# Attention of the meta tokens in layer 0: eight heads at a time in blocks of 16, instead of four in blocks of 32

## The chip, the cores and the metric

The kernel runs on one core of a Trainium2 chip. The metric is the time of one execution in microseconds on the device. The engines of a core work side by side, each through its own instructions in order: PE (matrix products), DVE (vector work), ACT (functions of one operand, and scaled copies), POOL (general work) and SP, which here only starts transfers.

## The reference

The reference is a decoder of two layers over 272 tokens (16 learned meta tokens, then 256 of the sequence), width 2048, 16 heads of 128. Layer 0 uses forgetting attention; the queries are taken in blocks, and the first block is the 16 meta tokens:

```
bounds = [(0, N_META)]                                  # 16 meta tokens
for start in range(N_META, total_len, BLOCK): ...       # then blocks of 128
s = einsum('bqhd,bkhd->bhqk', q[:, qs:qe], k[:, :qe]) * scale
s = s + cum_logf[:, :, qs:qe, None] - cum_logf[:, :, None, :qe]
p = softmax(where(k_pos <= q_pos, s, -inf))
o = einsum('bhqk,bkhd->bqhd', p, v[:, :qe])
```

So of every head the meta block is a product of 16 queries with 16 keys, a sum with differences of the forget gates, a softmax, and a product with 16 values. Then come the output projection and a squared-ReLU MLP of width 8192; layer 1 uses stick-breaking attention over keys and values shared from layer 0's output, and an MLP of its own. All is float32.

## The kernel before

Activations lie feature-major, x[feature, token], in 16 chunks of 128 features. Every large product (qkv, output projections, MLPs, shared k/v: 96 groups) runs through `gemm_group`: 512 columns of weights, four blocks `kb` of 512 features each. A block arrives as two halves `raw`; ACT writes each half rounded to the PE's faster float type (`whi`, L235), DVE writes what is left over (`wlo`, L236), and PE does three products for each pair of weight tile and chunk: whi with x's upper part, whi with its lower part, wlo with the upper part (L177). In layer 0 the moving operand is 272 columns wide, in most of layer 1 it is 256.

In layer 0 the heads go in four groups `g` of four heads. Each group has a q, a k and a v product; the attention's small work is put among them by hand through `before`, `after` and `mid`, and by a scheduler which orders the rest from a model of its own. `behind` fixes a small matmul behind the last large one, so that it stands at a set place in the PE's queue.

What concerns the meta tokens, for one group of four heads:

- L600: `packed` lets POOL copy the first 32 query columns of each head to a 128-column tile `qm`.
- `meta` (L603) runs ahead of block 2 of the v product. One full float32 matmul of `qm` with the first 32 key columns of four heads gives a 128x128 tile `ps0`, in which only the four 32x32 blocks on the diagonal count (L605); DVE makes the decays `s0` from the gates `fk`, the column `fqm_sb` and the mask `maskM` (L608), adds and takes the minimum (L610); ACT takes the exponential (L612); DVE divides (L613, L614).
- After the v product the first 32 value columns are turned to token-major: for groups 0 to 2 by DVE and 16 copies shared by ACT and POOL (`turned_corners`, L523 and L528; the last 16 keys of each 128-token block go along), for group 3 by two PE transposes (L635).
- `small` (L630) runs ahead of block 2 of the next product (of block 1 in the output projection): DVE turns the probabilities (L639), one full float32 matmul multiplies them with the values (`pom`, L641), and `put_split` writes the 16 real columns of four heads to the attention's output `ao` (L642).

`outputs` (L483) does the 128-token blocks; for group 3 it stands in the middle of block 2 of the first group of the output projection. Its matmuls `po` need the probabilities' parts `ph`, `pl` and the values' parts `vs` (upper part by ACT, L448, lower part by DVE, L449). The gates of the meta queries come from four small transfers that ACT starts (`meta_gates`, L373).

The activations `x` live in two buffers of 16 rows of 640 columns and 64 columns more.

Of the kernel before, what the change touches and what calls it, by code (L numbers as in the profile page):

```python
# [21 lines left out]
EPS = 1e-6  # L22
BIG = 1.0e30
# [4 lines left out]
SPAN = 6  # L28
WIDE = {"o1": (0, 4, 10)}
XROW = 640  # L30
# [6 lines left out]
def yoco_kernel(ctx: ExitStack, tc: tile.TileContext, hT_in, gains, b_f, w_f, w_qkv0, w_o0, w_up, w_dn,  # L37
                w_kv, w_q1, w_o1, g_fin, out):
    nc = tc.nc

    const = ctx.enter_context(tc.tile_pool(name="const", bufs=1))
# [4 lines left out]
    xs = ctx.enter_context(tc.tile_pool(name="xs", bufs=2))  # L46
    tmp = ctx.enter_context(tc.tile_pool(name="tmp", bufs=2))
# [19 lines left out]
    for _ in range(9):  # L67
# [12 lines left out]
    nc.gpsimd.affine_select(out=maskM, in_=maskM, compare_op=ALU.is_ge, fill=BIG, base=0,  # L80
                            pattern=[[-32, 4], [-1, 32]], channel_multiplier=1)
    nc.gpsimd.affine_select(out=maskM, in_=maskM, compare_op=ALU.is_ge, fill=BIG, base=31,
                            pattern=[[32, 4], [0, 32]], channel_multiplier=-1)


    maskB = const.tile([P, 416], F32, name="maskB")
# [18 lines left out]
    class Split:  # L105


        def __init__(self, label, t0):
            n = T - t0
            self.t0 = t0  # L110
            rows = xs.tile([P, NC * XROW + 64], F32R, tag="x", name=f"x_{label}")
            hi, lo = ROWS[t0]
            o = min(hi, lo)
            rows = rows[:, o:o + NC * XROW].rearrange("p (c t) -> p c t", c=NC)
            self.hi, self.lo = (rows[:, :, k - o:k - o + n] for k in (hi, lo))

            if t0:
                self.wide = {}
                self.wide_chunks = WIDE.get(label, (0,))
                for c in self.wide_chunks:  # L120
                    for name, k in (("hi", hi), ("lo", lo)):
                        nc.gpsimd.tensor_copy(rows[:, c, k - o + n:k - o + n + SPAN], pad[:, :SPAN])
                        self.wide[name, c] = rows[:, c, k - o:k - o + n + SPAN]

    def split_chunk(sp, gi, c):

# [177 lines left out]
    xa = Split("a0", 0)  # L304
# [14 lines left out]
            norm.add(c)  # L319

    fq_sb = const.tile([P, 2, NC], F32, name="fq_sb")
    fqm_sb = const.tile([P, 4], F32, name="fqm_sb")
    f_dram = tc.dram_tile([NC, T], F32, name="f_dram")

    def load_gates():
        wf_sb = att.tile([P, NC, NC], F32, tag="qs", name="wf_sb")
        wf = att.tile([P, NC, 2 * NC], F32, tag="qs", name="wf")
        for t, n, c, out, src in ((wf_sb[:, 0], P, 13, wf_sb, w_f), (bf_sb, NC, 14, bf_sb, b_f),
                                  (g_sb[:, 0], P, 15, g_sb, gains)):
            nc.gpsimd.tensor_copy(t[:n, :1], hT[:n, c, :1])  # L330
            nc.gpsimd.dma_start(out, src)
        nc.vector.memset(wf, 0.0)
        nc.vector.tensor_tensor(out=wf[:, :, :NC], in0=wf_sb, op=ALU.mult,
                                in1=g_a0.unsqueeze(2).to_broadcast([P, NC, NC]))
        both = att.tile([P, P], F32, tag="pk", bufs=3, name="both")[:, :NC]
# [33 lines left out]

    def meta_gates():  # L370

        for g in range(4):
            nc.scalar.dma_start(fqm_sb[:, g:g + 1], f_dram[4 * g:4 * g + 4, :32].rearrange("h (t o) -> h t o", o=1))  # L373

    def split_q(q, label):

# [127 lines left out]
    def packed(src, label):  # L504

        n = src.shape[2]
        t = att.tile([P, P], F32, tag="pk", bufs=3, name=f"pk_{label}")[:, :4 * n]
        nc.gpsimd.tensor_copy(t.rearrange("p (h t) -> p h t", h=4), src)
        return t

    def corners(a, b, label):

        t = att.tile([P, P], F32, tag="pk", bufs=3, name=f"pk_{label}")
        for i, src in enumerate((a, b)):
            nc.gpsimd.tensor_copy(t.rearrange("p (h c t) -> p h c t", h=4, c=2)[:, :, i, :], src)
        return t

    def turned_corners(parts, out, label):

        n = len(parts)  # L520
        ct = tmp.tile([P, T], F32, tag="u2", name=f"ct_{label}")[:, :n * P].rearrange("p (s k) -> p s k", s=n)
        for i, src in enumerate(parts):
            nc.vector.transpose(out=ct[:, i], in_=src)  # L523
        out = out.rearrange("p (s k) -> p s k", s=n)
        for a in range(0, P, 32):
            for b in range(0, P, 32):
                copy = nc.scalar.copy if n == 2 and a < 64 else nc.gpsimd.tensor_copy
                copy(out[b:b + 32, :, a:a + 32], ct[a:a + 32, :, b:b + 32])  # L528

    def last_keys(vT):  # L530

        return vT[:, :, M:].rearrange("p h (c t) -> p h c t", c=2)[:, :, :, P - M:]

    def put_split(sp, h, nh, t, n, src):
        hi, lo = (x[:, h:h + nh, t - sp.t0:t - sp.t0 + n] for x in (sp.hi, sp.lo))
        nc.scalar.activation(hi, src, AF.Copy)
        nc.vector.tensor_tensor(out=lo, in0=src, in1=hi.bitcast(F32), op=ALU.subtract)
# [3 lines left out]
    for g in range(4):  # L541
# [55 lines left out]
            for i, (o, n) in enumerate(((0, 144), (144, T))):  # L597
                nc.vector.tensor_scalar(s[:, j, o:o + n], s[:, j, o:o + n], st[:, 2 + i:3 + i], None, op0=ALU.mult)

        qm = packed(qT[:, :, :32], f"qm_{g}")  # L600
        s0 = tmp.tile([P, T], F32, tag="sq", name=f"s0_{g}")[:, :P]

        def meta(g=g, qm=qm, kT=kT, s0=s0, fk=fk, last=box["s"]):  # L603
            ps = patt.tile([P, 512], F32, tag="patt", name=f"ps0_{g}")
            behind(nc.tensor.matmul(ps[:, :P], qm, kT[:, :, :32], start=True, stop=True))  # L605
            st = att.tile([P, 4], F32, tag="st", name=f"st0_{g}")
            with tc.issue_after(last.ins):
                nc.vector.scalar_tensor_tensor(out=s0.rearrange("p (h k) -> p h k", h=4), in0=fk[:, :, :32],  # L608
                                               scalar=fqm_sb[:, g:g + 1], in1=maskM, op0=ALU.subtract, op1=ALU.add)
# [8 lines left out]

        vT, evac_v = values(f"0_{g}")
        plan = PLANS[0 if g else 2]  # L620
        gemm_group(w_qkv0[3 * g + 2], xa, 0, evac_v, {2: meta}, early(turn_p[0], plan[0]))

        if g == 3:
            vm, vc = packed(vT[:, :, 0:32], f"vm_{g}"), corners(vT[:, :, P:144], vT[:, :, 256:T], f"vc_{g}")
# [5 lines left out]
        def small(g=g, corner=(vm, vc) if g == 3 else None, vm_sb=vm_sb, sm=sm, s0=s0, box=box):  # L630
# [10 lines left out]
            behind(nc.tensor.matmul(po[:, :P], vm_sb[:, :P], pm_sb[:, P:], start=True, stop=True))  # L641
# [192 lines left out]

    def last_down(f, u):

        home = xs.tile([P, NC * XROW + 64], F32R, tag="x", name="home")[:, :8 * 1152].rearrange(
            "p (q h w k c) -> p q h w k c", q=2, h=2, w=2, k=2)
        for g in range(4):
            pool, tag = ((patt, "patt"), (pacc, "acc"))[g % 2]  # L840
# [82 lines left out]
```

## Time and profile before

| | |
|---|---|
| median of 3 runs | 2260.46 us (2260.19 to 2261.04) |
| the profiled execution | 2261.43 us, of which 2259.70 us are the span from its first to its last instruction |
| PE | 2250.6 us busy, 18845 matmuls |
| DVE | 1390.7 us busy (62%) |
| ACT | 1125.6 us busy (50%) |
| POOL | 112.4 us busy (5%) |
| memory | 408.33 MB read, 182 GB/s over the span |
| layer 0's attention and its projections | roughly the first 410 us |

A group of the profile is one line of the program on one engine with the tiles it writes and reads; behind the count stand the busy time, the mean length of one, and the idle time of the engine ahead of it. The length of a matmul reaches from its start to its end in the array, and the next one starts before that end; so what a matmul costs in a dense stream is read from the starts of its neighbours. A float32 matmul counts as two.

### The profile page before, as it was taken

Reading aid. Unit: us, or ns where it says so; the run is one execution under the profiler, and the core shown is the slowest. Engines: PE = TensorE matmul, PEld = TensorE weight load, DVE = VectorE, ACT = ScalarE, POOL = GpSimd, SP = SyncE. Lnnn points to the kernel's source line nnn. Section 1 sums busy time; section 2 is a strip of 40 time slices with the busy share of each in tenths; the row PEclk is TensorE's granted clock in tenths of the full one; section 3 lists DMA queues with packets and bytes.
Section 4 is the critical chain, followed back from the end, with each engine's and each line's share of the span. In section 5 each row is a group of like instructions: output and inputs, shape, how many; then the busy total and the mean of one; then the engine's idle time right before and its main releaser. Section 6 shows DMA issues by size and latency. Waiting matters only on the chain.

```text
span 2259.7 us, 44965 instructions
## 1 busy us (share of the span) xinstructions
PE 2250.6 (100%) x18845; PEld 2247.4 (99%) x18845; DVE 1390.7 (62%) x1997; ACT 1125.6 (50%) x1577; POOL 112.4 (5%) x220
## 2 busy tenths in 40 slices
PE   9999999999999999999999999999999999999998
PEld 9999999999999999999999999999999999999998
DVE  7877786554455455445566688876555555555655
ACT  6664565443344344344544577755543544543543
POOL 1000000000000000000000010100000000001421
PEclk9999999999999999999999999999999999999999
DMA  7545545555555555555555544466656656565564
GB/s 245 183 158 176 182 160 176 182 174 177 185 173 183 178 169 186 171 184 179 175 187 187 177 163 160 168 203 187 202 183 203 194 188 201 183 204 193 187 200 150
DMA packets 116507, 413.37 MB, mean 183 GB/s; under 512 B 13456, under 2 KB 15776, under 8 KB 116304
## 3 DMA queue, kind: packets, MB, share of 16 engines
q1 hardware_dynamic: 113904, 406.25, 55.4%
q8 instruction: 147, 2.41, 0.5%
q10 hardware_dynamic: 2000, 3.03, 0.4%
q0 software_dynamic: 400, 1.21, 0.1%
q14 instruction: 56, 0.46, 0.1%
HBM read 408.33 MB, written 2.11 MB: 182 GB/s over the span
## 4 chain that ended last, share of the span: by engine, by line
PE 99%; DMA 1%; DVE 0%; ACT 0%; issue 0%; DVEq 0%; ACTq 0%
PE acc L177 93%; PE acc_t L293 4%; DMA raw<-w_qkv 1%; PE ps L400 1%; PE po L495 1%; PE ps L398 0%; PE po L498 0%; DMA rows<-hT_in 0%; PE pf L344 0%; DVE wlo L236 0%; PE pc L486 0%; DVE x_a L132 0%; DVE ssq_a L149 0%; ACT x_a L131 0%; ACT whi L235 0%; PE ps L605 0%
## 5 line engine op out<-in xcount | busy, mean ns | idle before, releaser
L236 DVE TENSOR_TENSOR wlo<-raw,whi 128x1024 fp32r<-128x1024 f32 (+1 forms) x742 | 891.0, 1218 | 605.6 <-ACT whi L235 599.4
L235 ACT ACTIVATE whi<-raw 128x1024 fp32r<-128x1024 f32 (+1 forms) x742 | 764.5, 1050 | 881.7 <-PE acc L177 847.6
L177 PE MATMUL acc<-x_m,whi 128*128 128x272 f32 (+1 forms) x4096 | 642.6, 281 | 0.0
L177 PE MATMUL acc<-x_u,whi 128*128 128x272 f32 (+1 forms) x3584 | 576.6, 282 | 0.0
L177 PEld LDWEIGHTS acc<-x_m,whi 128*128 128x128 f32 x4096 | 565.7, 188 | 0.0
L177 PEld LDWEIGHTS acc<-x_u,whi 128*128 128x128 f32 x3584 | 504.0, 188 | 0.0
L177 PE MATMUL acc<-x_m,wlo 128*128 128x272 f32 (+1 forms) x2048 | 440.7, 281 | 0.0
L177 PE MATMUL acc<-x_u,wlo 128*128 128x272 f32 (+1 forms) x1792 | 403.9, 282 | 0.0
L177 PE MATMUL acc<-x_a,whi 128*128 128x272 f32 (+1 forms) x2048 | 352.8, 285 | 0.1
L177 PEld LDWEIGHTS acc<-x_m,wlo 128*128 128x128 f32 x2048 | 323.2, 188 | 0.0
L177 PEld LDWEIGHTS acc<-x_a,whi 128*128 128x128 f32 x2048 | 300.2, 188 | 1.3 <-issue 0.9
L177 PEld LDWEIGHTS acc<-x_u,wlo 128*128 128x128 f32 x1792 | 290.7, 188 | 0.0
L177 PE MATMUL acc<-x_a,wlo 128*128 128x272 f32 (+1 forms) x1024 | 252.8, 285 | 0.3 <-DVE wlo L236 0.3
L177 PE MATMUL acc<-x_kv,whi 128*128 128x272 f32 x1024 | 192.4, 287 | 0.0
L177 PEld LDWEIGHTS acc<-x_a,wlo 128*128 128x128 f32 x1024 | 175.6, 188 | 0.7 <-DVE wlo L236 0.7
L177 PE MATMUL acc<-x_o,whi 128*128 128x272 f32 (+2 forms) x1024 | 162.0, 282 | 0.0
L177 PEld LDWEIGHTS acc<-x_kv,whi 128*128 128x128 f32 x1024 | 160.0, 188 | 0.0
L177 PE MATMUL acc<-x_kv,wlo 128*128 128x272 f32 x512 | 147.1, 287 | 0.0
L177 PEld LDWEIGHTS acc<-x_o,whi 128*128 128x128 f32 x1024 | 141.8, 188 | 0.0
L177 PE MATMUL acc<-x_o,wlo 128*128 128x272 f32 (+1 forms) x512 | 110.2, 281 | 0.0
L300 DVE TENSOR_TENSOR rows<-acc,rows 128x272 f32<-128x272 f32 (+1 forms) x144 | 62.3, 433 | 74.1 <-PE acc L177 74.1
L177 PEld LDWEIGHTS acc<-x_kv,wlo 128*128 128x128 f32 x512 | 96.4, 188 | 0.0
(216 smaller groups left out, 1521.8 us busy)
## 6 DMA issues: line engine op xcount, KB each, us to landing
raw<-w_up SPq DMA_DIRECT2D x256, 512.0 KB, 3.9
raw<-w_dn SPq DMA_DIRECT2D x224, 512.0 KB, 3.7
raw<-w_qkv SPq DMA_DIRECT2D x92, 512.0 KB, 3.9
raw<-w_o SPq DMA_DIRECT2D x64, 512.0 KB, 4.0
raw<-w_kv SPq DMA_DIRECT2D x64, 512.0 KB, 3.8
raw<-w_q SPq DMA_DIRECT2D x32, 512.0 KB, 4.4
raw_t<-w_dn SPq DMA_DIRECT2D x32, 512.0 KB, 4.3
fk<-f_dram ACTq DMA_DIRECT2D x4, 544.0 KB, 5.5
```

The source lines that it names most:

```text
L177: ins = nc.tensor.matmul(*args, **kw).ins
L235: on_act = nc.scalar.activation(hp, src, AF.Copy)
L236: on_dve = nc.vector.tensor_tensor(out=lp, in0=src, in1=hp.bitcast(F32), op=ALU.subtract)
L293: ins = nc.tensor.matmul(accs[b][h][:, :256 + over], x[:, 4 * kb + kc, b * P:(b + 1) * P], parts[kc // 2][w][:, kc % 2, 256 * h:256 * h + ...
L300: nc.vector.tensor_tensor(out=hT[:, c, t0:], in0=acc, in1=hT[:, c, t0:], op=ALU.add)
L400: nc.tensor.matmul(ps[:, 144:416], qs[a][:, j, :], ks[b][:, j, :], start=i == 0, stop=i == 2)
L495: ins = nc.tensor.matmul(po[:, i, :], vk, pk, start=i == k == 0, stop=False)
```

## The change

The meta attention is done for two groups of four heads together, in 16-column blocks of eight heads, in the odd groups alone. Tiles `qm`, `km`, `vm` and `s0` of 8 x 16 columns are made once for a pair of groups; POOL fills their halves from `qT`, `kT` and `vT` (three copies of 64 columns a group, where one of 128 stood). The even groups keep only their half of the decays. So `ps0`, the softmax, the turning of values and probabilities, `pom` and `put_split` stand twice and not four times. In even groups `turned_corners` has one part and not two; its 16 copies then all go to POOL. `meta_gates` starts two transfers, not four. The pool `pk` has two buffers, not three, and the 64 spare columns of an `x` buffer go, so that the second `x` buffer starts 256 bytes earlier in a partition; the columns used within a buffer stay the same.

```diff
-    maskM = const.tile([P, 4, 32], F32, name="maskM")
+    maskM = const.tile([P, 8, M], F32, name="maskM")
...
-            rows = xs.tile([P, NC * XROW + 64], F32R, tag="x", name=f"x_{label}")
+            rows = xs.tile([P, NC * XROW], F32R, tag="x", name=f"x_{label}").rearrange("p (c t) -> p c t", c=NC)
             hi, lo = ROWS[t0]
-            o = min(hi, lo)
-            rows = rows[:, o:o + NC * XROW].rearrange("p (c t) -> p c t", c=NC)
-            self.hi, self.lo = (rows[:, :, k - o:k - o + n] for k in (hi, lo))
+            self.hi, self.lo = (rows[:, :, k:k + n] for k in (hi, lo))
...
-        for g in range(4):
-            nc.scalar.dma_start(fqm_sb[:, g:g + 1], f_dram[4 * g:4 * g + 4, :32].rearrange("h (t o) -> h t o", o=1))
+        for g in range(2):
+            nc.scalar.dma_start(fqm_sb[:, g:g + 1], f_dram[8 * g:8 * g + 8, :M].rearrange("h (t o) -> h t o", o=1))
...
-        qm = packed(qT[:, :, :32], f"qm_{g}")
-        s0 = tmp.tile([P, T], F32, tag="sq", name=f"s0_{g}")[:, :P]
-
-        def meta(g=g, qm=qm, kT=kT, s0=s0, fk=fk, last=box["s"]):
+        if g % 2 == 0:
+            qm, km, vm, s0 = (att.tile([P, 8, M], F32, tag=f"meta_{x}", bufs=1, name=f"{x}_{g}") for x in ("qm", "km", "vm", "s0"))
+        four = slice(4 * (g % 2), 4 * (g % 2) + 4)
+        nc.gpsimd.tensor_copy(qm[:, four], qT[:, :, :M])
+        nc.gpsimd.tensor_copy(km[:, four], kT[:, :, :M])
+
+        def meta_decays(g=g, s0=s0, fk=fk, last=box["s"], four=four):
+            with tc.issue_after(last.ins):
+                nc.vector.scalar_tensor_tensor(out=s0[:, four], in0=fk[:, :, :M], scalar=fqm_sb[:, g // 2:g // 2 + 1],
+                                               in1=maskM[:, four], op0=ALU.subtract, op1=ALU.add)
+
+        def meta(g=g, qm=qm, km=km, s0=s0, decays=meta_decays):
             ps = patt.tile([P, 512], F32, tag="patt", name=f"ps0_{g}")
-            behind(nc.tensor.matmul(ps[:, :P], qm, kT[:, :, :32], start=True, stop=True))
+            behind(nc.tensor.matmul(ps[:, :P], qm, km, start=True, stop=True))
...
-        gemm_group(w_qkv0[3 * g + 2], xa, 0, evac_v, {2: meta}, early(turn_p[0], plan[0]))
-
+        gemm_group(w_qkv0[3 * g + 2], xa, 0, evac_v, {2: meta if g % 2 else meta_decays}, early(turn_p[0], plan[0]))
+
+        nc.gpsimd.tensor_copy(vm[:, four], vT[:, :, :M])
...
-            turned_corners([vT[:, :, 0:32], last_keys(vT)], vm_sb, f"0_{g}")
+            turned_corners([vm, last_keys(vT)] if g % 2 else [last_keys(vT)], vm_sb if g % 2 else vm_sb[:, P:], f"0_{g}")
...
-            nc.vector.transpose(out=pm_sb[:, P:], in_=s0)
+            if g % 2 == 0:
+                return
+            nc.vector.transpose(out=pm_sb[:, P:], in_=s0.rearrange("p h k -> p (h k)"))
             po = patt.tile([P, 512], F32, tag="patt", name=f"pom_{g}")
             behind(nc.tensor.matmul(po[:, :P], vm_sb[:, :P], pm_sb[:, P:], start=True, stop=True))
-            put_split(ao, 4 * g, 4, 0, M, po[:, :P].rearrange("p (h q) -> p h q", h=4)[:, :, :M])
+            put_split(ao, 4 * g - 4, 8, 0, M, po[:, :P].rearrange("p (h q) -> p h q", h=8))
```

On PE, `ps0` and `pom` of the groups 0 and 2 are gone, and nothing stands in their place. Beside the instructions that go, the scheduler moves others at two places, shown below; the remaining order on PE is the same. On DVE and ACT a few more rows move in groups 1 and 2 (the turned values' copies on ACT stand behind `ph` in group 1, and DVE turns `vm` four rows after the last keys). The names below carry the numbers of a build; `acc_13` is the first group of the output projection, and the first number behind `whi` or `wlo` is that of the product (3 is the v product of group 0), the second its block, the third the half.

On ACT, from the gates' transfers of group 0 into its v product, before:

```order
L373 DMA fqm_sb_138<-f_dram_141 128x1x1 x4
L389 ACTIVATE kh0_0_581<-kT0_0_580 128x272 x3
L235 ACTIVATE whi_3_1_0_976<-raw_3_1_0_972 128x1024
L235 ACTIVATE whi_3_1_1_980<-raw_3_1_1_973 128x1024
L389 ACTIVATE kh0_0_581<-kT0_0_580 128x272
L235 ACTIVATE whi_3_2_0_1044<-raw_3_2_0_1040 128x1024
L235 ACTIVATE whi_3_2_1_1048<-raw_3_2_1_1041 128x1024
L594 ACTIVATE s_0_579,st_0_852<-s_0_579,st_0_852 128x144
L594 ACTIVATE s_0_579,st_0_852<-s_0_579,st_0_852 128x272
L594 ACTIVATE s_0_579,st_1_865<-s_0_579,st_1_865 128x144
L594 ACTIVATE s_0_579,st_1_865<-s_0_579,st_1_865 128x272
```

and now:

```order
L371 DMA fqm_sb_138<-f_dram_141 128x1x1 x2
L387 ACTIVATE kh0_0_579<-kT0_0_578 128x272 x3
L233 ACTIVATE whi_3_1_0_977<-raw_3_1_0_973 128x1024
L233 ACTIVATE whi_3_1_1_981<-raw_3_1_1_974 128x1024
L387 ACTIVATE kh0_0_579<-kT0_0_578 128x272
L592 ACTIVATE s_0_577,st_0_850<-s_0_577,st_0_850 128x144
L233 ACTIVATE whi_3_2_0_1038<-raw_3_2_0_1034 128x1024
L592 ACTIVATE s_0_577,st_0_850<-s_0_577,st_0_850 128x272
L592 ACTIVATE s_0_577,st_1_863<-s_0_577,st_1_863 128x144
L592 ACTIVATE s_0_577,st_1_863<-s_0_577,st_1_863 128x272
L233 ACTIVATE whi_3_2_1_1042<-raw_3_2_1_1035 128x1024
```

Two of the four transfers go, and the halves of block 2 now stand among the exponentials of the scores instead of ahead of them; DVE's subtraction `wlo_3_2_1` likewise moves behind the divisions of the first two heads, and the first score product with `kh` moves 10 large matmuls forward on PE.

On PE, in the middle of block 2 of the output projection's first group, where `outputs` of group 3 stands, before:

```order
L486 MATMUL pc_0_3_4213<-pm_sb_0_3_4083,vm_sb_3_4003 128x128
L177 MATMUL acc_13_0_4006<-x_o0_142,whi_13_2_1_4176 128x272 x2
L177 MATMUL acc_13_0_4006<-x_o0_142,wlo_13_2_1_4177 128x272
L177 MATMUL acc_13_0_4006<-x_o0_142,whi_13_2_1_4176 128x272 x2
L177 MATMUL acc_13_0_4006<-x_o0_142,wlo_13_2_1_4177 128x272
L177 MATMUL acc_13_1_4007<-x_o0_142,whi_13_2_1_4176 128x272
L495 MATMUL po_0_3_0_4216<-ph_0_3_4110,vs_0_3_4186 128x256
L495 MATMUL po_0_3_0_4216<-pl_0_3_4111,vs_0_3_4186 128x256
L495 MATMUL po_0_3_1_4228<-ph_0_3_4110,vs_0_3_4186 128x256
L495 MATMUL po_0_3_1_4228<-pl_0_3_4111,vs_0_3_4186 128x256
```

and now:

```order
L484 MATMUL pc_0_3_4191<-pm_sb_0_3_4061,vm_sb_3_3981 128x128
L493 MATMUL po_0_3_0_4194<-ph_0_3_4088,vs_0_3_4164 128x256
L493 MATMUL po_0_3_0_4194<-pl_0_3_4089,vs_0_3_4164 128x256
L493 MATMUL po_0_3_1_4206<-ph_0_3_4088,vs_0_3_4164 128x256
L493 MATMUL po_0_3_1_4206<-pl_0_3_4089,vs_0_3_4164 128x256
L175 MATMUL acc_13_0_3984<-x_o0_142,whi_13_2_1_4154 128x272 x2
L175 MATMUL acc_13_0_3984<-x_o0_142,wlo_13_2_1_4155 128x272
L175 MATMUL acc_13_0_3984<-x_o0_142,whi_13_2_1_4154 128x272
L493 MATMUL po_0_3_0_4194<-ph_0_3_4088,vs_0_3_4164 128x256
L496 MATMUL po_0_3_0_4194<-pt_0_3_3708,vt_0_3_3980 128x128
```

The four `po` matmuls that use the upper part of `vs` follow `pc` at once, where 7 large matmuls stood between; the first `po` that uses the lower part of `vs` (the ninth row) now has 4 large matmuls ahead of it since `pc`, where it had 16.

More of the change, by code (lines that the diff above doesn't have):

```diff
@@ L76, in yoco_kernel @@
                             base=M + P, pattern=[[-1, T]], channel_multiplier=1)
-    maskM = const.tile([P, 4, 32], F32, name="maskM")
+    maskM = const.tile([P, 8, M], F32, name="maskM")
     nc.gpsimd.memset(maskM, 0.0)
     nc.gpsimd.affine_select(out=maskM, in_=maskM, compare_op=ALU.is_ge, fill=BIG, base=0,
-                            pattern=[[-32, 4], [-1, 32]], channel_multiplier=1)
-    nc.gpsimd.affine_select(out=maskM, in_=maskM, compare_op=ALU.is_ge, fill=BIG, base=31,
-                            pattern=[[32, 4], [0, 32]], channel_multiplier=-1)
+                            pattern=[[-M, 8], [-1, M]], channel_multiplier=1)
+    nc.gpsimd.affine_select(out=maskM, in_=maskM, compare_op=ALU.is_ge, fill=BIG, base=M - 1,
+                            pattern=[[M, 8], [0, M]], channel_multiplier=-1)
     maskB = const.tile([P, 416], F32, name="maskB")
@@ L121, in __init__ @@
                     for name, k in (("hi", hi), ("lo", lo)):
-                        nc.gpsimd.tensor_copy(rows[:, c, k - o + n:k - o + n + SPAN], pad[:, :SPAN])
-                        self.wide[name, c] = rows[:, c, k - o:k - o + n + SPAN]
+                        nc.gpsimd.tensor_copy(rows[:, c, k + n:k + n + SPAN], pad[:, :SPAN])
+                        self.wide[name, c] = rows[:, c, k:k + n + SPAN]
     def split_chunk(sp, gi, c):
@@ L321, in yoco_kernel @@
     fq_sb = const.tile([P, 2, NC], F32, name="fq_sb")
-    fqm_sb = const.tile([P, 4], F32, name="fqm_sb")
+    fqm_sb = const.tile([P, 2], F32, name="fqm_sb")
     f_dram = tc.dram_tile([NC, T], F32, name="f_dram")
@@ L506, in packed @@
         n = src.shape[2]
-        t = att.tile([P, P], F32, tag="pk", bufs=3, name=f"pk_{label}")[:, :4 * n]
+        t = att.tile([P, P], F32, tag="pk", bufs=2, name=f"pk_{label}")[:, :4 * n]
         nc.gpsimd.tensor_copy(t.rearrange("p (h t) -> p h t", h=4), src)
@@ L511, in corners @@
     def corners(a, b, label):
-        t = att.tile([P, P], F32, tag="pk", bufs=3, name=f"pk_{label}")
+        t = att.tile([P, P], F32, tag="pk", bufs=2, name=f"pk_{label}")
         for i, src in enumerate((a, b)):
@@ L598, in yoco_kernel @@
                 nc.vector.tensor_scalar(s[:, j, o:o + n], s[:, j, o:o + n], st[:, 2 + i:3 + i], None, op0=ALU.mult)
-        qm = packed(qT[:, :, :32], f"qm_{g}")
-        s0 = tmp.tile([P, T], F32, tag="sq", name=f"s0_{g}")[:, :P]
-        def meta(g=g, qm=qm, kT=kT, s0=s0, fk=fk, last=box["s"]):
+        if g % 2 == 0:
[8 more added lines that the diff above has]
+        def meta(g=g, qm=qm, km=km, s0=s0, decays=meta_decays):
             ps = patt.tile([P, 512], F32, tag="patt", name=f"ps0_{g}")
-            behind(nc.tensor.matmul(ps[:, :P], qm, kT[:, :, :32], start=True, stop=True))
+            behind(nc.tensor.matmul(ps[:, :P], qm, km, start=True, stop=True))
             st = att.tile([P, 4], F32, tag="st", name=f"st0_{g}")
-            with tc.issue_after(last.ins):
-                nc.vector.scalar_tensor_tensor(out=s0.rearrange("p (h k) -> p h k", h=4), in0=fk[:, :, :32],
-                                               scalar=fqm_sb[:, g:g + 1], in1=maskM, op0=ALU.subtract, op1=ALU.add)
+            decays()
+            s0 = s0.rearrange("p h k -> p (h k)")
             nc.vector.tensor_tensor_reduce(out=s0, in0=ps[:, :P], in1=s0, scale=1.0,
@@ L627, in yoco_kernel, with small @@
         if g < 3:
-            turned_corners([vT[:, :, 0:32], last_keys(vT)], vm_sb, f"0_{g}")
-        def small(g=g, corner=(vm, vc) if g == 3 else None, vm_sb=vm_sb, sm=sm, s0=s0, box=box):
+            turned_corners([vm, last_keys(vT)] if g % 2 else [last_keys(vT)], vm_sb if g % 2 else vm_sb[:, P:], f"0_{g}")
+        def small(g=g, corner=(vm.rearrange("p h k -> p (h k)"), vc) if g == 3 else None, vm_sb=vm_sb, sm=sm, s0=s0, box=box):
             box["pm"] = pm_sb = corner_probs(sm, f"0_{g}")
@@ L835, in last_down @@
     def last_down(f, u):
-        home = xs.tile([P, NC * XROW + 64], F32R, tag="x", name="home")[:, :8 * 1152].rearrange(
+        home = xs.tile([P, NC * XROW], F32R, tag="x", name="home")[:, :8 * 1152].rearrange(
             "p (q h w k c) -> p q h w k c", q=2, h=2, w=2, k=2)
```

4 lines of the change are left out of this document (2 added, 2 removed).

## The prediction

> **What bounds the kernel now.** I read the cores' view first, then the page's busy times and chain, then PE's waits.
>
> ```profile
> core 0: 2259.7 us, clock 0.999
> PE 2250.6 (100%) x18845; PEld 2247.4 (99%) x18845; DVE 1390.7 (62%) x1997; ACT 1125.6 (50%) x1577; POOL 112.4 (5%) x220
> PE 99%; DMA 1%; DVE 0%; ACT 0%; issue 0%; DVEq 0%; ACTq 0%
> PE idle L68 <- DVE mean_w L62: 1.1, 1, 1.1
> PE acc L177 <- DVE wlo L236: 0.3, 1, 0.3
> ```
>
> PE is the bound: 99% of the chain that ends last is PE, it runs at its full granted clock (0.999), and its waits on other engines add up to 1.4 us. Time is won only by taking instructions out of PE's queue or by starting them closer together, and lost only if PE now waits for something or its matmuls start further apart. The meta tokens' work on DVE (62% busy), ACT (50%) and POOL (5%) costs nothing in itself.
>
> The profiled execution took 2261.43 us, of which 2259.70 are the span; the median of the runs shown, 2260.46, is 0.97 lower. I make the sum as a difference against the profiled execution and take it off the median.
>
> **What leaves PE.** Four full float32 matmuls go: `ps0` and `pom` of the groups 0 and 2. Of each of these two rows of the profile half goes:
>
> ```profile
> L641 PE MATMUL pom<-pm_sb,vm_sb 128*128 128x128 f32 x8 | 1.5, 272 | 0.0
> L605 PE MATMUL ps<-kT,pk_qm 128*128 128x128 f32 x8 | 1.5, 272 | 0.0
> ```
>
> Each matmul counts twice, so 8 records are four matmuls. What one costs is read from the starts around it, here in group 0's v product:
>
> ```profile
> 71.77 0.29 PE L177 MATMUL acc<-x_a,wlo 128*128 128x272 f32 x1
> ...
> 72.14 0.29 PE L177 MATMUL acc<-x_a,wlo 128*128 128x272 f32 x1
> 72.27 0.38 PE L605 MATMUL ps<-kT,pk_qm 128*128 128x128 f32 x2
> 72.40 0.50 PE L177 MATMUL acc<-x_a,whi 128*128 128x272 f32 x2
> 72.74 0.29 PE L177 MATMUL acc<-x_a,wlo 128*128 128x272 f32 x1
> 72.87 0.41 PE L177 MATMUL acc<-x_a,whi 128*128 128x272 f32 x2
> 73.11 0.29 PE L177 MATMUL acc<-x_a,wlo 128*128 128x272 f32 x1
> ```
>
> From one `wlo` to the next stand three large matmuls, 72.14 - 71.77 = 0.37 us (0.123 each); the stretch with `ps0` takes 72.74 - 72.14 = 0.60. So one small matmul costs 0.23 us of PE. `pom` has the same shape and the same 272 ns. Four of them are **-0.92 us**, all on the path, because PE never rests there.
>
> The Trainium skill (TensorE: Matmul & The Clock Gate, "Wait — 56ns, not 53.3ns?") has N / 2.4 GHz + about 2.5 ns for one warm matmul in a stream, 56 ns at 128 columns. By that page two passes would be 0.11 us and the four matmuls 0.45 us, an estimate, and the forecast 0.47 us later. The row above has twice that, and I take the row.
>
> **What is moved on PE, in the output projection.** `outputs` of group 3 now stands tighter behind `pc`. First PE, then DVE, then ACT, before the change:
>
> ```profile
> 329.35 0.38 PE L486 MATMUL pc<-pm_sb,vm_sb 128*128 128x128 f32 x2
> 329.49 0.49 PE L177 MATMUL acc<-x_o,whi 128*128 128x272 f32 x2
> ...
> 330.44 0.28 PE L495 MATMUL po<-ph,vs 128*128 128x256 f32 x1
> 330.56 0.28 PE L495 MATMUL po<-pl,vs 128*128 128x256 f32 x1
> ...
> 332.03 0.28 PE L495 MATMUL po<-ph,vs 128*128 128x256 f32 x1
> ...
> 332.29 0.36 PE L495 MATMUL po<-ph,vs 128*128 128x256 f32 x1
> 332.49 0.28 PE L495 MATMUL po<-pl,vs 128*128 128x256 f32 x1
> ...
> 334.87 0.46 PE L177 MATMUL acc<-x_o,whi 128*128 128x272 f32 x2
> ```
>
> ```profile
> 327.80 1.23 DVE L236 TENSOR_TENSOR wlo<-raw,whi 128x1024 fp32r<-128x1024 f32 x1
> 328.94 0.22 DVE L537 TENSOR_TENSOR x_o<-pom,x_o 128x64 fp32r<-128x64 f32 x1
> 329.07 1.22 DVE L236 TENSOR_TENSOR wlo<-raw,whi 128x1024 fp32r<-128x1024 f32 x1
> 330.20 0.69 DVE L449 TENSOR_TENSOR vs<-vt,vs 128x512 fp32r<-128x512 f32 x1
> ```
>
> ```profile
> 327.86 0.63 ACT L448 ACTIVATE vs<-vt 128x512 fp32r<-128x512 f32 x1 [0.34 <-DVE vt L441]
> ```
>
> The upper part of `vs` is there at 327.86 + 0.63 = 328.49, so the first four `po` may follow `pc` at once. The lower part comes at 330.20 + 0.69 = 330.89; DVE is dense ahead of it, and the row `x_o<-pom` now has 128 columns for 64, which I put at 0.07 more (a subtraction of 1024 columns takes 330.20 - 329.07 = 1.13 from start to start, so 64 take 0.07): 330.96. PE needs that part at the fifth `po`. In the old order that was 332.03, with 1.1 us to spare. In the new one it is 329.35, plus 0.14 for `pc` (329.49 - 329.35), 0.20 for the first `po` behind a float32 matmul (332.49 - 332.29), 3 x 0.12 for the next three (330.56 - 330.44) and 4 x 0.123: 330.54. All these times hang on the end of group 3's v product and move together. For handing over between the engines I allow 0.05; no row shows PE waiting for DVE at such a place. PE waits 330.96 + 0.05 - 330.54 = **+0.47 us**, with all later matmuls behind it.
>
> Something comes back. The old order has PE held a little at block 3, which needs what `outputs` wrote: the pair at 334.87 lasts 0.46, against 0.41 for a pair elsewhere (at 72.87). In the new one the `po` end about 0.9 us earlier, less the wait, and that hold goes: **-0.05**. The bounds of this part are 0 (the part arrives in time) and +0.6 (handing over takes 0.15).
>
> **What is moved in group 0.** The chain there starts with ACT:
>
> ```profile
> 54.78 3.13 ACTq L373 DMA_DIRECT2D fqm_sb<-f_dram  x4
> 57.96 1.07 ACT L389 ACTIVATE kh<-kT 128x272 fp32r<-128x272 f32 x3 [5.26 <-DMA fqm_sb<-f_dram]
> ...
> 61.02 0.38 PE L400 MATMUL ps<-kh,qh 128*128 128x272 f32 x1
> ```
>
> ```profile
> 65.68 0.30 DVE L591 CUSTOM_DVE_ANT_0 s<-ps,s 128x144 f32<-128x144 f32 x1
> ...
> 66.86 2.36 DVE L236 TENSOR_TENSOR wlo<-raw,whi 128x1024 fp32r<-128x1024 f32 x2
> 69.13 0.41 DVE L596 RECIPROCAL st<-st 128x2 f32<-128x2 f32 x2
> 69.46 1.03 DVE L598 TENSOR_SCALAR s<-s,st 128x144 f32<-128x144 f32 x4
> ```
>
> Starting the four transfers keeps ACT for 3.13 us; two take about half, so `kh` can come some 1.5 us earlier. The first product with `kh` stands 10 x 0.123 = 1.2 us earlier on PE, near 59.8; even the old `kh` starts at 57.96 and its first third is done by about 58.4. No wait. The second half of block 2, `wlo_3_2_1`, was done at 66.86 + 2.36 = 69.22. It now follows the divisions (0.41 + 1.03) and one more head's pair of score rows, about 0.6 (two heads take 66.86 - 65.68 = 1.18), and its `whi` stands behind exponentials; with 1 us more for those it is done by 72.3. PE needs it 24 large matmuls into block 2, at 72.40 + 24 x 0.123 = 75.35, less 0.23. I take 0, with 3 us of cover; if the cover were gone, each late half would be paid in full, +0.5 to +1.5.
>
> **What costs nothing.** The 64-column copies on POOL (5% busy) lie a whole product ahead of `ps0` and `pom`; DVE's turning of `vm` in group 1 waits for POOL, with the subtractions of the weights queued behind it, but four turns of the values stand ahead of it as cover. If POOL came later than these, DVE's slack on the weights would pay first.
>
> **The sum.** -0.92 + 0.47 - 0.05 = -0.50 us. Against the profiled execution that is 2260.93; off the median, 2260.46 - 0.50 = **2260.0 us**. That is 0.02%, far inside the 0.2% (4.5 us) that a measurement of this kernel can tell from no change.
>
> **The rivals.**
>
> *The lower part of `vs` is in time.* If DVE's dense stretch ahead of it ends 0.5 us sooner, the whole saving stays: -0.92 - 0.05, 2259.5. For it: DVE loses small work in the groups 0 and 2. Against it: in group 3 its rows are as many as before. Chance 0.22.
>
> *Group 0 stalls.* If the exponentials hold up `whi` longer than I allow, PE waits for `wlo` in block 2 or 3: 2260.5 to 2261.5. For it: ACT and DVE are reordered there most. Against it: 3 us of cover. Chance 0.09.
>
> *POOL holds up DVE.* In groups 0 and 2 POOL now makes 16 copies where it made 8:
>
> ```profile
> 86.66 3.10 POOL L528 COPY vm_sb<-ct 32x64 f32<-32x64 f32 x8 [10.06 <-DVE ct L523]
> ```
>
> Eight took 3.10 us beside DVE's subtractions. Were DVE to stand still for as long in each of the two groups, it would lose some 3 us twice, about the cover that I found for the weights in group 0; PE might pay 0.5, giving 2260.5. It decides only where the loss exceeds that cover. Chance 0.04. The Trainium skill (SBUF — State Buffer, "Who interferes with whom") states the rule that speaks for this: a DVE instruction with two SBUF inputs contends with a GpSimd instruction that reads SBUF, and the later one waits. The row agrees that something waits: eight copies in 3.10 us are 0.39 each; it does not show DVE waiting.
>
> *Matmuls start further apart: slower.* The second `x` buffer moves by 256 bytes, and PE has a slower gait, seen in layer 1 behind a float32 matmul:
>
> ```profile
> 1469.99 1.08 PE L177 MATMUL acc<-x_o,whi 128*128 128x262 f32 x8
> 1470.90 0.27 PE L769 MATMUL pvc<-ident,pk_vc 128*128 128x128 f32 x1
> 1470.93 1.19 PE L177 MATMUL acc<-x_o,whi 128*128 128x262 f32 x8
> 1471.96 1.09 PE L177 MATMUL acc<-x_o,wlo 128*128 128x262 f32 x8
> ...
> L177 PE MATMUL acc<-x_m,whi 128*128 128x256 f32 x2032 | 262.5, 276 | 0.0
> ```
>
> Eight matmuls ahead of `pvc` take 1470.90 - 1469.99 = 0.91 (0.114 each); the eight behind it 1471.96 - 1470.93 = 1.03, of which the first is 0.20, so the others 0.118 each: 0.0045 more. It outweighs the saving from about 110 matmuls on and shows in the time from 1,000 on. Should layer 1's up projections, which read the second buffer (the 2032 of the last row and half as many with `wlo`), keep that gait throughout, they cost 3048 x 0.0045 = 14 us: 2274. Against it: the gait ended within those eight, and the columns within a buffer stay. Chance 0.04. The same shift could as well bring starts closer together (0.03 for faster by over 0.2%), though no row shows a quicker gait.
>
> **How the numbers follow.** 2260.0 has 0.58; the rivals 0.22, 0.09, 0.04, 0.04 and 0.03. The first four cases all lie within 0.2%: same 0.93, slower 0.04, faster 0.03. The range covers 2259.5 less, and 2261.5 more, some 0.4 to 0.7 for the scatter of the runs (2260.19 to 2261.04): 2258.8 to 2261.9.
>
> **What would show it.** Right: `ps0` and `pom` with x4 records each; 0.37 us between `wlo` starts across block 2 of group 0; one new wait of PE, `po` for DVE's `vs`, near 0.5 us; the first pair of block 3 at 0.41. Wrong: no such wait (the first rival), a wait of `acc` for `wlo` below 90 us (the second) or in the groups' next products (the third), or more than 0.125 between the large matmuls of 272 columns, 0.115 of 256, over hundreds of them.

## The result, and the profile after

| | before | after |
|---|---|---|
| median of 22 runs each | 2260.47 us (2259.34 to 2261.91) | 2263.34 us (2261.41 to 2265.57) |
| ratio after / before | | 1.0014, 95% interval 1.0007 to 1.0020 |
| profiled execution's span | 2259.70 us | 2261.5 us |

The changed kernel is 2.9 us slower, where the forecast was 0.5 us faster. The removal itself took place. The groups of the profile show `ps0` and `pom` with half their records:

```profile
L611 PE MATMUL ps<-km,qm 128*128 128x128 f32 x4 | 0.8, 274 | 0.0
L649 PE MATMUL pom<-pm_sb,vm_sb 128*128 128x128 f32 x4 | 0.8, 272 | 0.0
```

The cores' view and the page's busy times of the changed kernel:

```profile
core 0: 2261.5 us, clock 0.998
PE 2249.9 (99%) x18837; PEld 2246.9 (99%) x18837; DVE 1387.7 (61%) x1983; ACT 1120.4 (50%) x1555; POOL 129.7 (6%) x243
```

PE is busy 0.7 us less and yet the span is longer. What PE waits for (engine, tile and line, what it waits for; then us in total, times, longest):

```profile
PE acc L175 <- DVE x_o L535: 2.6, 1, 2.6
PE idle L68 <- DVE mean_w L62: 1.1, 1, 1.1
```

The first row is new: one stop of 2.6 us, on a large matmul that needs what DVE writes into `x_o`. It has its place in the timeline of PE, at the start of block 2 of the output projection's first group (start, length, instruction; in brackets how long PE stood idle ahead of it, and what ended that):

```profile
321.60 0.38 PE L649 MATMUL pom<-pm_sb,vm_sb 128*128 128x128 f32 x2
...
323.92 0.28 PE L175 MATMUL acc<-x_o,whi 128*128 128x272 f32 x1
326.82 0.39 PE L175 MATMUL acc<-x_o,whi 128*128 128x272 f32 x1 [2.62 <-DVE x_o L535]
327.06 0.28 PE L175 MATMUL acc<-x_o,wlo 128*128 128x272 f32 x1
...
328.33 0.66 PE L175 MATMUL acc<-x_o,whi 128*128 128x272 f32 x2
328.79 0.43 PE L175 MATMUL acc<-x_o,wlo 128*128 128x272 f32 x1
329.01 0.66 PE L175 MATMUL acc<-x_o,whi 128*128 128x272 f32 x2
```

DVE and ACT at the same place:

```profile
322.62 2.69 DVE L439 STREAM_TRANSPOSE vt<-vT 32x256 f32<-32x256 f32 x6
325.35 1.23 DVE L234 TENSOR_TENSOR wlo<-raw,whi 128x1024 fp32r<-128x1024 f32 x1
326.49 0.28 DVE L535 TENSOR_TENSOR x_o<-pom,x_o 128x128 fp32r<-128x128 f32 x1
```

```profile
322.02 0.28 ACT L534 ACTIVATE x_o<-pom 128x128 fp32r<-128x128 f32 x1
```

`pom` of group 3 is done near 322.0, and ACT writes the upper part at once. The lower part stands on DVE behind six turns and a subtraction of weights and is done at 326.49 + 0.28 = 326.77. The second matmul of block 2 reads it and starts at 326.82 in place of 323.92 + 0.12 = 324.04: 2.78 us late. Block 2 holds the features 1024 to 1535, which are heads 8 to 11. Before the change their meta columns came from group 2, and DVE had written them 72 us earlier:

```profile
254.26 0.22 DVE L537 TENSOR_TENSOR x_o<-pom,x_o 128x64 fp32r<-128x64 f32 x1
```

Now one `put_split` writes heads 8 to 15 together, when group 3 is ready.

The stop has a second cost. In the timeline, three large matmuls take 329.01 - 328.33 = 0.68 us, where three took 0.37. The table by stretches (length; busy time and count of PE, its weight loads PEld, DVE, ACT, POOL; PE's granted clock; share and GB/s of the transfers) shows why:

```profile
326.82:328.17 1.35, 1.34 (x11) 1.35 (x12) 1.35 (x2) 0.00 (x0) 0.00 (x0) 1.00 0.40 94
328.22:331.63 3.41, 3.41 (x17) 3.41 (x17) 0.28 (x1) 0.51 (x1) 0.00 (x0) 0.50 0.78 272
```

From 328.22 on, 1.40 us behind the stop, PE has half its clock for 3.41 us, and each large matmul costs 0.227 us in place of 0.123.

Both traces have the same 18,432 large matmuls in the same order, so the start of each in one trace can be taken from its start in the other. The table gives how this distance to the first trace of before grows in each stretch (us; negative is ahead; times are those of before), for all kernels of this study:

| trace | to 46 us | 46 to 326.4 | 326.4 to 326.7 (the stop) | 326.7 to 336 | 336 to 1470 | 1470 to 1490 | to the end |
|---|---|---|---|---|---|---|---|
| after | -1.55 | -0.91 | +2.89 | +1.50 | 0.00 | 0.00 | -0.28 |
| e0, after again | -1.55 | -0.91 | +3.05 | +1.14 | 0.00 | 0.00 | -0.28 |
| before again | -1.24 | 0.00 | 0.00 | 0.00 | +0.01 | 0.00 | -0.28 |
| e1, early write | -0.31 | -0.91 | 0.00 | +0.51 | 0.00 | 0.00 | -0.28 |
| e4, half as late | -1.47 | -0.91 | +1.75 | -0.06 | 0.00 | 0.00 | -0.28 |
| e5, late write alone | -1.46 | 0.00 | +2.94 | +1.48 | 0.00 | +1.55 | -0.28 |
| e3, early write, late po | -1.82 | -0.91 | 0.00 | -0.09 | 0.00 | 0.00 | -0.28 |
| e6, groups 0 and 1 only | -1.25 | -0.45 | 0.00 | 0.00 | +0.01 | 0.00 | -0.28 |
| e7, filler, first execution | +0.09 | -0.91 | +2.42 | +1.30 | 0.00 | 0.00 | -0.28 |
| e7, second execution | -1.07 | -0.91 | +2.24 | +1.49 | 0.00 | 0.00 | -0.28 |
| e7, third execution | -0.23 | -0.91 | +2.25 | -0.06 | 0.00 | +1.37 | -0.28 |
| e4, second execution | -1.09 | -0.91 | +1.75 | -0.07 | 0.00 | +1.04 | -0.28 |

The first, the sixth and the last column belong to single executions: the second trace of the unchanged kernel differs from its first one by 1.24 and 0.28 there. What the change did lies in the three columns between: -0.91 for the four matmuls, and +4.38 (after) or +4.19 (e0) at block 2. Whether the change also moves the start by some tenths of a microsecond, these single executions cannot tell.

### The profile page after: what moved, and what is told of

Its sections match the earlier page's. It is cut to its first block, busy times and chain, and to the rows that moved or that the text cites. A ratio compares the mean times of both kernels' runs of the same rounds, so it can differ in the third digit from the quotient of the medians.

```text
span 2261.5 us, 44929 instructions
## 1 busy us (share of the span) xinstructions
PE 2249.9 (99%) x18837; PEld 2246.9 (99%) x18837; DVE 1387.7 (61%) x1983; ACT 1120.4 (50%) x1555; POOL 129.7 (6%) x243
## 4 chain that ended last, share of the span: by engine, by line
PE 85%; DVE 0%; ACT 0%; DVEq 0%; issue 0%
PE acc L175 80%; PE acc_t L291 4%; PE po L493 0%; PE ps L398 0%; PE po L496 0%; PE ps L396 0%; PE pc L484 0%; DVE hrow L840 0%; DVE hrow L838 0%; DVE hrow L811 0%; DVE sqr L814 0%; ACT sums L824 0%; DVEq L927 0%; PE pms_m L156 0%; PE pms_m L155 0%; DVE sums L827 0%
```

## The experiments

**e0: the changed kernel again.**

> The changed kernel once more, unaltered. Theory: block 2 of the first group of the output projection reads heads 8 to 11 of the attention's output, whose meta columns are now written together with those of heads 12 to 15, late; PE stops 2.7 us there and then runs some 3 us at half its clock (+1.5 us). Expected 2262.3 to 2264.5, the same stop near 326.8 us, and the stretch at half clock either there again or begun at another moment. Rival: the time is spread over the whole run, and the stop or the half clock does not come back.

2263.18 us against 2260.25 (ratio 1.0012, 1.0003 to 1.0021). The stop is there again, of the same length. So is the half clock, but it begins at 326.44, while PE still stands, and not 1.40 us behind the stop, so that the first matmul is slow already:

```profile
326.44:326.82 0.38, 0.00 (x1) 0.01 (x1) 0.38 (x3) 0.00 (x0) 0.00 (x0) 0.50 0.18 75
```

```profile
326.82 0.59 PE L175 MATMUL acc<-x_o,whi 128*128 128x272 f32 x1 [2.61 <-DVE x_o L535]
327.21 0.43 PE L175 MATMUL acc<-x_o,wlo 128*128 128x272 f32 x1
```

The loss belongs to the kernel, not to one execution.

**e1: the late write moved ahead, alone.** The lower part of the meta output goes ahead of the last six turns and of block 3's weights on DVE. The `po` are fixed on PE where the changed kernel has them, so that PE's and ACT's order are the same as there.

```diff
-            put_split(ao, 4 * g - 4, 8, 0, M, ...)
+            box["mo"] = put_split(ao, 4 * g - 4, 8, 0, M, ...)   # returns the lower part's instruction
...
+        if g == 3:
+            def last_turns(piece=turning[2]):
+                with tc.issue_after(box["mo"].ins):
+                    piece()
+            turning[2] = last_turns
...
+                        if hold and kb == 3:                     # first group of the output projection
+                            held.enter_context(tc.issue_after(hold["mo"].ins))
                         on_dve = nc.vector.tensor_tensor(out=lp, in0=src, in1=hp.bitcast(F32), op=ALU.subtract)
```

> The changed kernel with one row moved on DVE: the lower part of the meta output of heads 8 to 15 is written two entries (six turns of the values and one subtraction of weights) earlier. PE's and ACT's order stay. Theory: the write is done near 322.9, block 2 starts unheld at 324.05, there is no half clock, and what is left is the wait of the first lower po for vs that the prediction named, 0.3 to 0.5: 2260.46 - 0.92 + 0.4 = 2259.9 (2259.3 to 2260.8). Rival, the loss lies elsewhere (copies on POOL, addresses, start): about 2263. Rival, the wait moves on to what was moved back (weights of block 3, vs): 2261 to 2262.

2259.67 us against 2260.25 (0.9997, 0.9989 to 1.0006). One row of DVE moved by two entries takes back the whole loss: 3.5 us between e0 and e1, measured side by side. Its waits:

```profile
PE idle L68 <- DVE mean_w L62: 1.1, 1, 1.1
PE po L517 <- DVE vs L456: 0.3, 1, 0.3
PE acc L175 <- DVE wlo L241: 0.3, 1, 0.3
```

The stop at block 2 is gone; the last row is one that a trace of before has too. What comes up is the wait that the prediction named, on PE and DVE:

```profile
329.20 0.29 PE L175 MATMUL acc<-x_o,whi 128*128 128x272 f32 x1
329.80 0.39 PE L517 MATMUL po<-ph,vs 128*128 128x256 f32 x1 [0.32 <-DVE vs L456]
330.03 0.38 PE L518 MATMUL po<-pt,vt 128*128 128x128 f32 x2
```

```profile
323.74 0.29 DVE L580 TENSOR_TENSOR x_o<-pom,x_o 128x128 fp32r<-128x128 f32 x1
...
329.06 0.69 DVE L456 TENSOR_TENSOR vs<-vt,vs 128x512 fp32r<-128x512 f32 x1
```

The first lower `po` starts 0.60 us behind the matmul ahead of it, where 0.12 is usual: 0.48 us, with `vs` done at 329.75 and 0.05 for handing over. The next start comes 0.23 later and not 0.12, another 0.11.

**e4: half as late.** As e1, but the write stands behind the six turns and only ahead of block 3's weights (the wrapper `last_turns` is left out).

> The changed kernel with the same write only one entry earlier on DVE: behind the six turns, ahead of the subtraction of block 3's weights. It is then done 1.14 us earlier than in the changed kernel, and PE should stop 1.5 us in place of 2.7. Theory with the clock falling after any stop of this kind: 2260.46 - 0.92 + 1.5 + 1.5 = 2262.5. Theory with the clock falling only after a longer stop: 2261.0, no slice at half clock. Rival, the write is not what PE waits for: 2263.3, unchanged.

2260.70 us against 2260.25 (1.0002, 0.9994 to 1.0011). The stop follows the write, which is done at 325.42 + 0.29 = 325.71, 0.05 ahead of PE's new start:

```profile
325.42 0.29 DVE L580 TENSOR_TENSOR x_o<-pom,x_o 128x128 fp32r<-128x128 f32 x1
```

```profile
324.00 0.28 PE L175 MATMUL acc<-x_o,whi 128*128 128x272 f32 x1
325.76 0.40 PE L175 MATMUL acc<-x_o,whi 128*128 128x272 f32 x1 [1.48 <-DVE x_o L580]
326.00 0.29 PE L175 MATMUL acc<-x_o,wlo 128*128 128x272 f32 x1
```

There is no half clock behind it, so the version of the theory in which any stop of this kind brings the clock down is wrong. The wait for `vs` has vanished inside the stop, so e4 loses 1.75 - 0.06 = 1.69 by the table and e1 0.51, a difference of 1.18; the medians differ by 1.03.

**e5: the late write on the unchanged kernel.** All eight `ps0` and `pom` stay. The meta output of group 2 is copied to SBUF by ACT and written into `ao` right behind that of group 3.

```diff
+            if g == 2:
+                nc.scalar.copy(keep, mo)
+                return
+            hi, lo = put_split(ao, 4 * g, 4, 0, M, mo)
+            if g == 3:
+                with tc.issue_after(hi.ins), tc.issue_after(lo.ins):
+                    put_split(ao, 8, 4, 0, M, keep)
```

> The kernel before, with nothing of the change but the late write: the meta output of heads 8 to 11 is kept in SBUF by ACT and written into the attention's output behind that of heads 12 to 15. All eight ps0 and pom stay. Theory: PE stops near 326.5 for 2.7 to 3.3 us and runs at half clock for some us behind it: 2260.46 + 3.0 + 1.5 = 2265.0 (2263.2 to 2266). Rival, the cause is another part of the change: 2260.5.

2264.55 us against 2260.25 (1.0016, 1.0007 to 1.0025). Nothing else of the change is in the program, and the loss is there: +2.94 for the stop and +1.48 behind it.

```profile
327.48 0.22 DVE L537 TENSOR_TENSOR x_o<-pom,x_o 128x64 fp32r<-128x64 f32 x1
327.61 0.21 DVE L537 TENSOR_TENSOR x_o<-keep,x_o 128x64 fp32r<-128x64 f32 x1
```

```profile
327.88 0.39 PE L177 MATMUL acc<-x_o,whi 128*128 128x272 f32 x1 [2.67 <-DVE x_o L537]
```

One thing came along: here too the scheduler draws the `po` forward on PE, into the order of the changed kernel.

```profile
332.38 0.38 PE L486 MATMUL pc<-pm_sb,vm_sb 128*128 128x128 f32 x2
332.52 0.36 PE L495 MATMUL po<-ph,vs 128*128 128x256 f32 x1
```

So the late write by itself is enough for that move of the `po`, which the prediction priced as a part of the change. It stands behind the stop and is not the cause of the loss: e4 has the same order of the `po` and, at full clock, loses nothing there (-0.06).

**e3: both waits taken away.** e1, with `pc` where it was and all `po` ten large matmuls behind it.

> As e1 (the meta output's lower part two entries earlier on DVE), and all po now stand behind 10 large matmuls after pc, the first four too. Theory: the lower part of vs is ready at the fifth po, so the last wait goes, and with it the hold at block 3 (0.07): PE's starts from there on lie 0.98 us ahead of the kernel before (0.91 for the four matmuls), 0.58 ahead of e1: about 2259.1 to 2259.3. Rival, all po in one lump bring a wait of their own (the addition to po on DVE, x_o for block 3): 2259.7 or more, with a row of it among PE's waits.

2259.11 us against 2260.18 (0.9995, 0.9987 to 1.0004). PE's only wait left is that of the start:

```profile
PE idle L68 <- DVE mean_w L62: 1.1, 1, 1.1
```

By the table it is 1.00 us ahead of before at block 2 and stays so. It beats both kernels in the traces and in the medians, though the interval of its runs still holds 1.

**e6: the pairing for groups 0 and 1 only.** Groups 2 and 3 each do their own `ps0` and `pom`, in tiles of which the other half is set to zero (its decays to the mask's value), so heads 8 to 11 are written a product early again; the `po` stand as before the change.

```diff
-        gemm_group(w_qkv0[3 * g + 2], xa, 0, evac_v, {2: meta if g % 2 else meta_decays}, ...)
+        gemm_group(w_qkv0[3 * g + 2], xa, 0, evac_v, {2: meta if g else meta_decays}, ...)
...
-            put_split(ao, 4 * g - 4, 8, 0, M, ...)
+            put_split(ao, 0, 8, 0, M, mo) if g == 1 else put_split(ao, 4 * g, 4, 0, M, mo[:, four])
```

> The pairing for groups 0 and 1 alone; groups 2 and 3 do their own meta attention as before (in tiles of 8 x 16 of which the other half is zero), so heads 8 to 11 are written a product early again. PE's order around the po is that of before. Theory: two of the four matmuls go, nothing waits: 2260.25 - 0.46 = 2259.8 (2259.3 to 2260.3), no new wait of PE, no half clock. Rival, the copies on POOL and the other order in groups 0 and 1 cost PE something: above 2260.3.

2260.09 us against 2260.18 (0.9998, 0.9989 to 1.0007). Two matmuls less, -0.45, and no new wait. The pairing of groups 0 and 1 costs PE nothing; of the two pairs, only the one whose heads are needed at once does. The interval of the runs is too wide to show the 0.45.

**e7: between e4 and the changed kernel.** One subtraction of 416 columns stands on DVE ahead of the write.

```diff
+            ins = nc.vector.tensor_tensor(out=maskA, in0=maskA, in1=..., op=ALU.subtract)   # 128 x 416, not read again
+            with tc.issue_after(ins.ins):
                 nc.vector.tensor_tensor(out=lo, in0=src, in1=hi.bitcast(F32), op=ALU.subtract)
```

> As e4, with one more subtraction of 416 columns on DVE between the turns and the write (it spoils a mask that nothing reads any more): the write comes about 0.45 us later, and PE should stop 1.5 + 0.45 = 1.95 us. It tells from what length of stop on the clock falls. If it is the length alone, with the point between 1.5 and 1.95: a slice at half clock in the profile and 2260.7 + 0.45 + 1.4 = 2262.5. If the point lies between 1.95 and 2.6: 2261.1, full clock. If it is chance by the moment at which the stop falls: runs of both kinds, 2261 and 2262.5.

2261.68 us against 2260.18 (1.0007, 0.9998 to 1.0016), with six runs from 2260.83 to 2261.68 and five from 2262.50 to 2264.18. Two more executions of e7 were profiled, and one more of e4:

> e7 once more, for its profile. In its runs the time lay at 2260.8 to 2261.7 six times and at 2262.5 to 2264.2 five times; the profiled one, 2264.2, had the half clock. If the moment of the stop decides, a look with a time below 2262 has the same stop of 2.0 us and no slice at half clock; if the length decides, every look has the half clock and the faster times come from the start of the run alone.

> As e7_look2: a third look at the same kernel. Half clock with about 2262.5 or more, or full clock with about 2261.

> e4 once more, for its profile: a stop of 1.5 us. If stops of that length never bring the clock down, full clock and 2260.3 to 2262; a slice at half clock would show that the moment alone decides.

They took 2263.04, 2263.70 and 2262.00 us; as single runs these carry the disturbances of the table's first and sixth column. The clock is read from the stretches behind the stop: first, second and third execution of e7, then the second of e4.

```profile
328.00:329.00 1.00, 1.00 (x5) 1.00 (x6) 1.00 (x2) 0.00 (x0) 0.00 (x0) 0.50 0.21 86
```

```profile
328.00:329.00 1.00, 1.00 (x6) 1.00 (x6) 1.00 (x2) 0.00 (x0) 0.00 (x0) 0.50 0.21 53
```

```profile
328.00:329.00 1.00, 1.00 (x11) 1.00 (x10) 1.00 (x2) 0.00 (x0) 0.00 (x0) 1.00 0.09 37
```

```profile
328.00:329.00 1.00, 1.00 (x11) 1.00 (x10) 0.97 (x2) 0.00 (x0) 0.00 (x0) 1.00 0.72 176
```

The same kernel with the same stop had half the clock in two executions and full clock in the third; the stops of the second and the third are alike to 0.01 us:

```profile
326.66 0.39 PE L175 MATMUL acc<-x_o,whi 128*128 128x272 f32 x1 [1.97 <-DVE x_o L583]
```

```profile
327.51 0.40 PE L175 MATMUL acc<-x_o,whi 128*128 128x272 f32 x1 [1.98 <-DVE x_o L583]
```

So it is not the length alone that decides. The granted clock in the traces shows what goes with it. All five stretches at half clock behind a stop last 3.41 us, and every execution, with such a stretch or without, falls to half clock once more at its end, when PE is done (at 2256.75 us in the trace of after). From the first fall to this last one it is 1928.53 us in two executions and 1931.94 in three: 565 and 566 times 3.4133 us. So the clock changes on a grid of 3.41 us, whose place differs from execution to execution. For the three executions whose clock did not fall at the stop, the grid's place there is counted back from the last fall (2258.39, 2253.74 and 2255.88 us, in the order of the table). Cut at the grid, the stops look like this (us):

| execution | PE starts again | length of the stop | step of the grid in or behind the stop | the stop cut at the grid | half clock |
|---|---|---|---|---|---|
| after | 326.82 | 2.62 | 324.80 | 0.60 + 2.02 | from 328.22 |
| e0 | 326.82 | 2.61 | 326.44 | 2.23 + 0.38 | from 326.44 |
| e5 | 327.88 | 2.67 | 328.40 | 2.67 | from 328.40 |
| e7, first | 327.84 | 1.99 | 327.84 | 1.99 | from 327.84 |
| e7, second | 326.66 | 1.97 | 327.50 | 1.97 | from 327.50 |
| e7, third | 327.51 | 1.98 | 326.44 | 0.91 + 1.07 | none |
| e4, first | 325.76 | 1.48 | 325.21 | 0.93 + 0.55 | none |
| e4, second | 326.15 | 1.48 | 327.35 | 1.48 | none |

In all eight the clock fell at the end of a period of the grid in which PE had stood still for 1.97 us or more, and did not where the most in one period was 1.48. This was read from the traces afterwards; no run was made to test it, and where the limit lies between 1.48 and 1.97 is open.

Expecting the time below 2262 for the execution at full clock was wrong: the third one lost 1.37 us near 1,480 us, where ACT came late to a half of the weights. In e5, which lost 1.55 us there, the trace names a transfer as what ACT waited for:

```profile
1482.22 1.06 ACT L235 ACTIVATE whi<-raw 128x1024 fp32r<-128x1024 f32 x1 [3.21 <-DMA raw<-w_o]
```

It is not part of the change: other executions of e4 and e7 do not show it, nor does any of before or after.

## Why the prediction was wrong

**The step that failed** is the one on `x_o<-pom` in the paragraph on the output projection. It took that row as load alone: 128 columns for 64, 0.07 us more on DVE ahead of `vs`. It did not ask who reads what the row writes. The sum then took for granted that block 2 finds its operand ready, and named only block 3 as waiting for `x_o`. None of the rivals held the case, and the range left no room for it. The rows were at hand: before the change DVE wrote the last four heads' part at 328.94 + 0.22 = 329.16, and block 2's second matmul, which needs it in the new pairing, started at 326.51 (first and second in this row of before):

```profile
326.39 0.41 PE L177 MATMUL acc<-x_o,whi 128*128 128x272 f32 x2
```

With the prediction's own 0.07 for the wider row and 0.05 for handing over, 329.16 + 0.12 - 326.51 = 2.77 us; measured were 2.78. e5 shows this cause alone, e1 its cure.

**The half clock** adds 1.3 to 1.5 us (in e0 0.16 of it stands in the column of the stop, 3.05 for 2.89). No row of before shows PE stopping there, so its price could only be read afterwards. By the columns of the table the whole is -0.91 + 2.89 + 1.50 = +3.5 (after) and +3.3 (e0); the medians gave +2.9 both times. The rest may be executions in which the clock did not fall: a stop of 2.6 us can be cut by the grid into two parts that are both below 1.97. Both traces of the changed kernel have the half clock, so that stays open.

**The four matmuls** were right: -0.91 for -0.92, at the four places, 0.229 each. e6 has half of it. The figure of the Trainium skill (TensorE: Matmul & The Clock Gate, "Wait — 56ns, not 53.3ns?") would have given 0.45 for the four, an estimate; the starts around each removed matmul decide for the row. That estimate gave 0.056 us to each of the two records of such a matmul; in the trace of before the second record of the one at 72.27 starts at 72.37, 0.10 us behind the first.

**The wait for `vs`** was right in mechanism and size, but not in the changed kernel: there PE comes to it so late that `vs` is long done. Where the stop is gone (e1) it is 0.48 + 0.11 for starting again, less the 0.06 that comes back up to block 3 (as in e4): about 0.5 net, 0.51 by the table, for the forecast 0.42. The rival that `vs` is in time falls with it, and e1's -0.91 + 0.51 = -0.40 is what the sum of -0.50 foresaw without the missed stop.

**Group 0** does not stall: at the end of its v product the distance differs from that at 46 us only by the removed matmul. **POOL** takes longer than the rival put it, and PE does not feel it. These are the 16 copies of group 0 together, then two of the 16 one by one, and DVE beside the first of these two:

```profile
84.61 6.75 POOL L526 COPY vm_sb<-ct 32x32 f32<-32x32 f32 x16 [0.18 <-DVE ct L521]
84.86 1.11 POOL L526 COPY vm_sb<-ct 32x32 f32<-32x32 f32 x1
...
86.00 0.20 POOL L526 COPY vm_sb<-ct 32x32 f32<-32x32 f32 x1
```

```profile
84.65 1.25 DVE L234 TENSOR_TENSOR wlo<-raw,whi 128x1024 fp32r<-128x1024 f32 x1
```

Three of the 16 run beside subtractions of weights on DVE and take 1.11 to 1.27 us; the other 13 take 0.20 each. The subtractions keep their length (1.23 on average over the whole kernel). So here it is POOL that waits and not DVE, the other way round than the rival had it.

**The gait** (the distance from one large matmul to the next) adds up to the same within 0.01 us over the whole stretch from 336 to 1,470 us and on to 2,230, so the moved `x` buffer costs nothing.

**The bound of 0.2%** for what can be told from no change was too wide: 22 runs each gave an interval of 0.07% to either side, and the loss of 0.14% stands outside it.

## What to carry to other kernels

When small results are batched to save instructions, the batch is ready when its last member is. Follow each early member to its first reader, and set the new time of writing, with all that is queued ahead of the write on its engine, against the start of that reader. A write that had 72 us of cover can have less than none, and the repair may be one row's place in a queue and not the batch.

## What the runs showed of the hardware

- A stop of PE can cost more than its length: behind it the granted clock fell to 0.50 for 3.41 us in five of eight traces (after, e0, e5, two of e7), at 1.3 to 1.5 us each. It fell from 0.38 us before to 1.40 us after PE had started again, on a grid of 3.41 us, where 1.97 us or more of the stop lay in one period of the grid; with at most 1.48 in one period (one of e7, both of e4) it did not. The Trainium skill (TensorE: Matmul & The Clock Gate, "Part 1: The HAM clock gate (the "warmup" mystery)") has a free-running window of about 3.4 us, and half rate after at least one idle window. The grid in the traces agrees with such a window; that 1.97 us of standing still is enough, well short of a whole one, does not.
- The first matmul behind a stop holds up the next by about 0.11 us at full clock: 326.00 - 325.76 = 0.24 between starts in e4, against 0.12.
- A copy of 32 columns on POOL took 0.20 us, and 1.11 to 1.27 beside a subtraction of weights on DVE, which took its usual 1.2.
- From 46 us on, PE's starts repeat from execution to execution of one kernel to about 0.01 us, but for the half clock, which begins at varying moments, and single disturbances (near 1,480 and 2,231 us). Effects of half a microsecond are told from the starts in two traces, where medians of eleven runs cannot tell them.
